# Linear attention: a stacked fp32r gate product, 512-column decay sums, and a moved transpose of y

## The chip, the cores and the metric

The kernel runs on one core of a Trainium2 chip. The metric is the device time of one execution in microseconds (us); lower is better. A core has a matrix engine (TensorE, in profiles PE, its weight loads PEld), a vector engine (VectorE, DVE), a scalar engine (ScalarE, ACT), GpSimd (POOL) and SyncE (SP). Each engine works through its own stream of instructions in order and waits on semaphores for the others. DMA transfers are issued from the queues of SP, ACT and POOL. Matrix products are written to PSUM, a small memory of eight banks of 2 KB for each of 128 partitions; everything else lies in SBUF.

## What is computed

One layer of a streaming encoder is applied to a prompt of 2048 rows and a sample of 32 rows, 1024 channels wide. The mixing part has two branches that are fed by one input projection: banded softmax attention, and gated linear attention (GLA) with 4 heads, keys of 64 and values of 128. A gated MLP with a short convolution follows. The change touches only the linear attention:

```python
log_a = jax.nn.log_sigmoid((gk_low @ p['w_gk2'] + p['b_gk']).astype(jnp.float32)) / GK_NORM
...
cum = jnp.cumsum(ab, axis=2)
cum_end = cum[:, :, -1:]
q_t = qb * jnp.exp(cum) * (dk ** -0.5)
k_t = kb * jnp.exp(-cum)
k_end = kb * jnp.exp(cum_end - cum)
att = jnp.einsum('bnthk,bnshk->bnhts', q_t, k_t) * mask
o_intra = jnp.einsum('bnhts,bnshv->bnthv', att, vb)
upd = jnp.einsum('bnshk,bnshv->bnhkv', k_end, vb)
...
yb = rmsnorm(yb, p['g_gla']) * jax.nn.silu(gb.reshape(b, t, H_B, DV_B))
```

A low-rank product with 16 rows (gk_low) and a bias give a gate for each key channel. Sums of its logarithm over the rows of a block give decays, by which q and k are multiplied. Scores inside a block, a state that is carried on, and a normalisation per head follow.

## The kernel before

The whole program is one Python function, encoder_step. Stages follow each other: the input projection, then the stage of this case, then banded attention, gates and output projection, then the MLP. Of the engines' streams TensorE's is written out by hand (line 82: the order of the code is the order of the stream). On the other engines the framework orders instructions itself. Pools give buffers: bufs is the number of buffers for each tag, and a tile that takes over a buffer waits until the users of the one before are through.

Floating point products of full precision are made in two ways. An F32 operand goes in as it is, and such a product appears in the trace as two TensorE instructions. Or an operand is split into a rounded upper part of type F32R and the rest (split, line 67: a ScalarE copy and a VectorE subtraction), and mm3 (line 74) adds up three products, high by high, high by low and low by high. The projection of q and k of the banded attention does the latter, with 416 columns a product.

**The stage (lines 605 to 830).** Two streams are interleaved on TensorE. One is the generator dense, here qk_stream: 8 groups of weight columns by 5 blocks of 416 rows by 8 steps; one pull is one step, three fp32r products. After each eighth pull a block is complete; t_evac casts it (qh on ScalarE, ql on VectorE) and stores it. The other stream consists of 17 generators gla_chunk(c), for 128 rows each (the last for the 32 sample rows). Each has ten pieces, between the yields. They are numbered here:

1. load of the gate rows gk (L645);
2. transpose of gk to PSUM, and a VectorE copy into the tile gl (L648, L649); row 16 of gl is one and meets the bias row of wgk;
3. loads of v, of the output gate, of q and k; the gate product gl by wgk (L659), and the logarithm of the sigmoid, split into ah and al (L664 to L673);
4. and 5. for p=0 and p=1 (two heads each): the decay sums, products of ah and al with the constant 0/1/-1 matrix cm, in two sets of 320 columns (256 and 128 for the sample rows), each in a PSUM tile ex of the pool pE with two buffers (L682, L683); exponentials into E on ScalarE (L684, L685); decayed copies of k on GpSimd (kd) and VectorE (ke), and of q on VectorE (qd, qi) (L691 to L708);
6. and 7. for p=0 and p=1: scores (L720, L724) into the single tile pa, masked copies into at (L726 to L730), transpose of ke and its copy (L732, L734);
8. and 9. for p=0 and p=1: output products into po (L741, L745) and state update (L750, L753); after p=1 the normalised and gated y (ScalarE L761 to L763, VectorE L764 to L768);
10. transpose of y, a copy, and the store to ybT (L773 to L776).

The pool pM has two buffers, which all of the tiles pz, pz2, ptk, pu and pty use in turn. The columns of cm in order: sums from the block's start up to a row (128), sums from behind a row to the end (128), two coarser levels (64 and 32 rows), and differences against the middle of each 32 rows, 128 columns each.

The loop of lines 811 to 829 sets the order: in step c, cur is chunk c, nxt is c+1, after is c+2, load is c+3. In the order of TensorE the pieces are: 6 of cur; 2 pulls; 3 of nxt; 2 pulls; 7 of cur; 4 pulls; 8 of cur and 4 of nxt; 3 pulls; 9 of cur, 5 of nxt, 2 of after, 1 of load; 6 pulls; 10 of cur.

Of the kernel before, what the change touches and what calls it, by code (L numbers as in the profile page):

```python
# [58 lines left out]
def encoder_step(ctx: ExitStack, tc: tile.TileContext, I, O):  # L59
# [545 lines left out]
    with ExitStack() as st:  # L605
        stq = pool(st, "stgQ", bufs=2)
        gp = pool(st, "gla")
        pE = pool(st, "psE", bufs=2, space=PSUM)
        pA = pool(st, "psA", space=PSUM)
        pM = pool(st, "psM", bufs=2, space=PSUM)  # L610
# [3 lines left out]
        cm = gp.tile([128, 640], F32R, name="cm")  # L614
        cmr = gp.tile([128, 640], F32, name="cmr", tag="E0")
        nc.sync.dma_start(cmr, I["cmat"])
# [5 lines left out]
        wgk = gp.tile([128, 256], F32, name="wgk")  # L622
        nc.vector.memset(wgk, 0.0)
        nc.sync.dma_start(wgk[:17], I["wgk"])
# [10 lines left out]
        gl = gp.tile([128, 128], F32, name="glt")  # L635
        nc.vector.memset(gl, 1.0)

        def gla_chunk(c):
# [10 lines left out]
            nc.vector.tensor_copy(gl[:16, :n], pz[:16, 256:256 + n])  # L649
# [27 lines left out]
            for p in range(2):  # L677
                E = gp.tile([128, 768], F32, name="E", tag=f"E{p}")
                sets = [(0, 256), (512, 640)] if sample else [(0, 320), (320, 640)]
                for a, e in sets:  # L680
                    ex = pE.tile([128, 512], F32, name="ex", tag="ex")
                    nc.tensor.matmul(ex[:, :e - a], ah[:n, 128 * p:128 * p + 128], cm[:n, a:e], start=True, stop=False)  # L682
                    nc.tensor.matmul(ex[:, :e - a], al[:n, 128 * p:128 * p + 128], cm[:n, a:e], start=False, stop=True)  # L683
                    nc.scalar.activation(E[:, a:e], ex[:, :e - a], AF.Exp, scale=1.0 / 16)  # L684
                nc.scalar.activation(E[:, 640:768], ex[:, 512 - a:640 - a], AF.Exp, scale=-1.0 / 16)  # L685
# [5 lines left out]
                nc.gpsimd.tensor_mul(kd[:, :n], k, E[:, 640:640 + n])  # L691
                for j in range(2):
                    hs = slice(64 * j, 64 * j + 64)
                    nc.vector.tensor_mul(qd[hs, p, j, 0:n], q[hs], E[hs, 512:512 + n])
                    if not sample:
                        nc.vector.tensor_mul(qd[hs, p, j, 128:192], q[hs, 64:128], E[hs, 320:384])
# [3 lines left out]
                            E[hs, 384:512].rearrange("p (s c) -> p s c", s=2)[:, :, 32:64])  # L700
                if not sample:
                    nc.gpsimd.tensor_mul(kd[:, 128:192], k[:, 0:64], E[:, 256:320])
# [108 lines left out]
        for c in range(17):  # L811
            cur, nxt, after, load = chunks[c:c + 4]
            step(cur)
            pull(qk_stream, 2)
            step(nxt)
            pull(qk_stream, 2)
            step(cur)
# [1519 lines left out]
```

## Time and profile before

| | us |
|---|---|
| median of 3 runs | 3160.59 (3157.12 to 3160.79) |
| the profiled execution | 3162.02 |
| its span, first to last instruction | 3160.3 |
| VectorE busy in the span | 2239.8 (71%) |
| ScalarE busy in the span | 1648.8 (52%) |
| GpSimd busy in the span | 269.4 (9%) |

All times of the trace come from that one execution and count from the start of its span. A row of the groups or of the order of time names line, engine, operation, and the tiles it writes and reads, with the shape as partitions by elements. Durations of matmuls are modelled, and matmuls that follow each other overlap in the records. Queues, such as ACTq, are the engine's issuing of transfers.

### The profile page before, as it was taken

To read this page: it belongs to the slowest core of one execution; us is meant where nothing else is said; L and a number is where in the kernel's file an instruction comes from. 1 tells how busy PE (TensorE), PEld (TensorE's weight loads), DVE (VectorE), ACT (ScalarE), POOL (GpSimd) and SP (SyncE) were. 2 spreads that over 40 slices of the span, in tenths; PEclk is the share of its full clock that TensorE was granted. 3 is DMA by queue.
4 is the path that set the end of the run, shared out by engine and by line. 5 is a ranking of instruction groups with operands and counts; after the bars stand their busy time and mean duration, and the time that the engine had idled before them with its cause. 6 is when DMAs were issued, how large, how long until landed. Compare 5 with 4: busy or idle time off the path is not lost. (4 is left out here: it accounts for less than half of the span.)

```text
span 3160.3 us, 56426 instructions
## 1 busy us (share of the span) xinstructions
PE 3047.7 (96%) x19748; PEld 2947.7 (93%) x19748; DVE 2239.8 (71%) x4879; ACT 1648.8 (52%) x3792; POOL 269.4 (9%) x427
## 2 busy tenths in 40 slices
PE   6999999999999999999999999999999999999997
PEld 4899999998999999988999899999999999999997
DVE  6735617774555555566677799998888778897877
ACT  4522224443555555544454655567666556576755
POOL 2201201112111111120000000000000000000001
PEclk9999999999999999999999999999999999999998
DMA  7354435554433334575457686788897667888784
GB/s 220 91 156 125 139 98 142 137 137 128 130 109 111 107 100 117 169 230 184 140 175 227 211 256 210 223 256 225 249 265 217 189 189 230 263 250 284 242 267 146
DMA packets 598478, 580.12 MB, mean 184 GB/s; under 512 B 53201, under 2 KB 526530, under 8 KB 598194
## 3 DMA queue, kind: packets, MB, share of 16 engines
q1 hardware_dynamic: 553026, 527.86, 56.2%
q10 hardware_dynamic: 44432, 47.34, 4.7%
q8 instruction: 155, 2.54, 0.3%
q0 software_dynamic: 736, 1.33, 0.2%
q14 instruction: 129, 1.06, 0.1%
HBM read 388.71 MB, written 187.65 MB: 182 GB/s over the span
## 5 line engine op out<-in xcount | busy, mean ns | idle before, releaser
L1882 PE MATMUL ad<-hA,hB 128*128 128x350 f32 (+2 forms) x1734 | 301.7, 324 | 3.8 <-DVE hB L1824 2.4
L1882 PEld LDWEIGHTS ad<-hA,hB 128*128 128x128 f32 x1734 | 282.5, 189 | 5.5 <-DVE hB L1824 3.3
L78 PE MATMUL pm<-hA,wh 128*128 128x416 f32 x768 | 287.4, 374 | 0.0
L79 PE MATMUL pm<-hA,wh 128*128 128x416 f32 x768 | 269.3, 351 | 0.0
L80 PE MATMUL pm<-hA,wl 128*128 128x416 f32 x768 | 269.3, 351 | 0.0
L1824 DVE TENSOR_TENSOR hA<-raws,hA 128x512 fp32r<-128x512 f32 (+1 forms) x367 | 241.9, 668 | 13.0 <-ACT hA L1819 12.7
L1819 ACT ACTIVATE hA<-raws 128x512 fp32r<-128x512 f32 (+1 forms) x367 | 222.0, 617 | 29.9 <-DMA raws<-in_w_up_dram 11.1
L1882 PE MATMUL ad<-hA,hA 128*128 128x348 f32 (+2 forms) x1308 | 225.5, 323 | 2.5 <-ACT work L2008 1.8
L1882 PE MATMUL g<-hA,hB 128*128 128x348 f32 (+2 forms) x1248 | 217.1, 323 | 6.4 <-ACT work L2004 3.5
L1882 PEld LDWEIGHTS ad<-hA,hA 128*128 128x128 f32 x1308 | 211.8, 188 | 3.9 <-ACT work L2008 2.4
L1882 PEld LDWEIGHTS g<-hA,hB 128*128 128x128 f32 x1248 | 202.3, 188 | 9.1 <-ACT work L2004 4.7
L1882 PE MATMUL ad<-hA 128*128 128x350 f32 (+2 forms) x1173 | 205.1, 324 | 4.2 <-DVE hA L1734 4.1
L1882 PEld LDWEIGHTS ad<-hA 128*128 128x128 f32 x1173 | 191.7, 190 | 5.0 <-DVE hA L1734 4.4
L1824 DVE TENSOR_TENSOR hB<-raws,hB 128x512 fp32r<-128x512 f32 (+1 forms) x289 | 190.9, 668 | 6.5 <-ACT hB L1819 6.1
L1819 ACT ACTIVATE hB<-raws 128x512 fp32r<-128x512 f32 (+1 forms) x289 | 175.8, 617 | 25.3 <-DMA raws<-in_w_up_dram 11.8
L69 ACT ACTIVATE pth<-pp 128x256 fp32r<-128x256 f32 (+1 forms) x288 | 106.4, 373 | 139.2 <-PE pp L1027 135.9
L72 DVE TENSOR_TENSOR ptl<-pp,pth 128x256 fp32r<-128x256 f32 (+1 forms) x288 | 118.1, 414 | 85.2 <-ACT pth L69 82.4
L78 PE MATMUL pn<-wh,hA 128*128 128x256 f32 (+1 forms) x624 | 176.9, 283 | 0.0
L79 PE MATMUL pn<-wl,hA 128*128 128x256 f32 (+1 forms) x624 | 176.3, 283 | 0.0
L80 PE MATMUL pn<-wh,hA 128*128 128x256 f32 (+1 forms) x624 | 176.1, 282 | 0.0
L1991 ACT COPY g<-ad 128x348 f32<-128x348 f32 (+2 forms) x102 | 44.3, 434 | 244.1 <-PE ad L1882 156.4
L1882 PE MATMUL g<-hA,hA 128*128 128x350 f32 (+2 forms) x894 | 157.4, 325 | 4.0 <-ACT g L1991 2.3
(507 smaller groups left out, 8468.6 us busy)
## 6 DMA issues: line engine op xcount, KB each, us to landing
raws<-in_w_up_dram SPq DMA_DIRECT2D x220, 256.0 KB, 4.3
raws<-sW SPq DMA_DIRECT2D x176, 256.0 KB, 3.8
sW<-raws SPq DMA_DIRECT2D x88, 256.0 KB, 3.6
raws<-in_w_down_dram SPq DMA_DIRECT2D x80, 256.0 KB, 5.2
wr<-in_w_in_dram SPq DMA_DIRECT2D x76, 256.0 KB, 3.2
sgT<-tx ACTq DMA_DIRECT2D x80, 208.0 KB, 1.9
wa<-in_w_ada_dram SPq DMA_DIRECT2D x64, 256.0 KB, 3.0
keys<-ks SPq DMA_DIRECT2D x128, 128.0 KB, 2.9
```

The source lines that it names most:

```text
L69: i = nc.scalar.activation(hi, src, AF.Copy)
L72: nc.vector.tensor_sub(lo, src, f32(hi))
L78: nc.tensor.matmul(out, ah, bh, start=first and i == 0, stop=False)
L79: nc.tensor.matmul(out, ah, bl, start=False, stop=False)
L80: nc.tensor.matmul(out, al, bh, start=False, stop=last and i == n - 1)
L1819: act = nc.scalar.activation(hi[:, :n], raw(i, n), AF.Copy)
L1824: nc.vector.tensor_sub(lo[:, :n], raw(i, n), f32(hi[:, :n]))
L1882: nc.tensor.matmul(out[:, :w], l_[:, k], r_[:, k, :w], start=first and k == 0 and i == 0, stop=k == n - 1 and i == 2, skip_group_check=True)
L1991: nc.scalar.copy(g[:, 0, :w], ad[:, 0, :w])
```

## The change

Four edits, all in the stage described above.

The gate product: wgk holds three copies of the 17 rows, at partitions 0, 32 and 64: the upper part of the weights twice and their rest once. gl holds the upper part of the gate rows at 0, their rest at 32, the upper part again at 64. One fp32r product then adds up the three products. In piece 2 the transposed rows are copied once from PSUM (gz); two ScalarE copies and a VectorE subtraction fill gl.

The decay sums: the second group of 128 columns is dropped from cm, and the remaining 512 are made in one set, for the sample chunk too. What the dropped columns gave, the decay from a row to the block's end, now comes from a third exponential with a bias tb, the whole block's sum. The order of the columns in E changes with that. The pool pE has one buffer.

The order: piece 10 of chunk c moves into step c+1, behind 6 of cur, 3 of nxt and 2 pulls; 3 of nxt now directly follows 6 of cur.

Buffers: pM has three.

```diff
--- before.py
+++ after.py
@@ -605,23 +605,30 @@
     with ExitStack() as st:
         stq = pool(st, "stgQ", bufs=2)
         gp = pool(st, "gla")
-        pE = pool(st, "psE", bufs=2, space=PSUM)
+        pE = pool(st, "psE", space=PSUM)
         pA = pool(st, "psA", space=PSUM)
-        pM = pool(st, "psM", bufs=2, space=PSUM)
+        pM = pool(st, "psM", bufs=3, space=PSUM)
         pO = pool(st, "psO", space=PSUM)
 
 
-        cm = gp.tile([128, 640], F32R, name="cm")
-        cmr = gp.tile([128, 640], F32, name="cmr", tag="E0")
-        nc.sync.dma_start(cmr, I["cmat"])
+        cm = gp.tile([128, 512], F32R, name="cm")
+        cmr = gp.tile([128, 512], F32, name="cmr", tag="E0")
+        nc.sync.dma_start(cmr[:, 0:128], I["cmat"][:, 0:128])
+        nc.sync.dma_start(cmr[:, 128:512], I["cmat"][:, 256:640])
         nc.vector.tensor_copy(cm, cmr)
         cmask = gp.tile([128, 128], U8, name="cmask")
         cmf = gp.tile([128, 128], F32, name="cmf", tag="qi0")
         nc.sync.dma_start(cmf, I["cmask"])
         nc.vector.tensor_copy(cmask, cmf)
-        wgk = gp.tile([128, 256], F32, name="wgk")
-        nc.vector.memset(wgk, 0.0)
-        nc.sync.dma_start(wgk[:17], I["wgk"])
+        wgk = gp.tile([128, 256], F32R, name="wgk")
+        wgf = gp.tile([128, 256], F32, name="wgf", tag="e1")
+        wgh = gp.tile([128, 256], F32R, name="wgh", tag="ah")
+        nc.vector.memset(wgf, 0.0)
+        for r in (0, 32, 64):
+            nc.sync.dma_start(wgf[r:r + 17], I["wgk"])
+        nc.vector.tensor_copy(wgk[0:64], wgf[0:64])
+        nc.vector.tensor_copy(wgh[64:128], wgf[64:128])
+        nc.vector.tensor_sub(wgk[64:128], wgf[64:128], f32(wgh[64:128]))
         SBP, SBS = [], []
         for p in range(2):
             for x, sb in (("P", SBP), ("S", SBS)):
@@ -632,8 +639,9 @@
         nc.vector.memset(qd, 0.0)
         at = gp.tile([128, 2, 2, 128], F32, name="att")
         nc.gpsimd.memset(at, 0.0)
-        gl = gp.tile([128, 128], F32, name="glt")
-        nc.vector.memset(gl, 1.0)
+        gl = gp.tile([128, 128], F32R, name="glt")
+        for r, v in ((0, 1.0), (32, 0.0), (64, 1.0), (96, 0.0)):
+            nc.vector.tensor_scalar(gl[r:r + 32], onef[r:r + 32], v, None, op0=OP.mult)
 
         def gla_chunk(c):
 
@@ -646,7 +654,11 @@
             yield
             pz = pM.tile([128, 512], F32, name="pz", tag="pm")
             nc.tensor.transpose(pz[:16, 256:256 + n], gk[:n], ident[:n, :n])
-            nc.vector.tensor_copy(gl[:16, :n], pz[:16, 256:256 + n])
+            gz = gp.tile([16, 128], F32, name="gz")
+            nc.vector.tensor_copy(gz[:, :n], pz[:16, 256:256 + n])
+            nc.scalar.activation(gl[0:16, :n], gz[:, :n], AF.Copy)
+            nc.scalar.activation(gl[64:80, :n], gz[:, :n], AF.Copy)
+            nc.vector.tensor_sub(gl[32:48, :n], gz[:, :n], f32(gl[0:16, :n]))
             yield
             vb = gp.tile([128, 512], F32, name="vb", tag="vb", bufs=2)
             nc.sync.dma_start(vb[:n], vn[t0:t0 + n, 512:1024])
@@ -676,35 +688,36 @@
             EX, QI, KE, KD_ = [], [], [], []
             for p in range(2):
                 E = gp.tile([128, 768], F32, name="E", tag=f"E{p}")
-                sets = [(0, 256), (512, 640)] if sample else [(0, 320), (320, 640)]
-                for a, e in sets:
-                    ex = pE.tile([128, 512], F32, name="ex", tag="ex")
-                    nc.tensor.matmul(ex[:, :e - a], ah[:n, 128 * p:128 * p + 128], cm[:n, a:e], start=True, stop=False)
-                    nc.tensor.matmul(ex[:, :e - a], al[:n, 128 * p:128 * p + 128], cm[:n, a:e], start=False, stop=True)
-                    nc.scalar.activation(E[:, a:e], ex[:, :e - a], AF.Exp, scale=1.0 / 16)
-                nc.scalar.activation(E[:, 640:768], ex[:, 512 - a:640 - a], AF.Exp, scale=-1.0 / 16)
+                ex = pE.tile([128, 512], F32, name="ex", tag="ex")
+                nc.tensor.matmul(ex, ah[:n, 128 * p:128 * p + 128], cm[:n], start=True, stop=False)
+                nc.tensor.matmul(ex, al[:n, 128 * p:128 * p + 128], cm[:n], start=False, stop=True)
+                tb = gp.tile([128, 1], F32, name="tb", tag=f"tb{p}")
+                nc.scalar.activation(tb, ex[:, n - 1:n], AF.Copy, scale=1.0 / 16)
+                nc.scalar.activation(E[:, 0:512], ex, AF.Exp, scale=1.0 / 16)
+                nc.scalar.activation(E[:, 512:640], ex[:, 384:512], AF.Exp, scale=-1.0 / 16)
+                nc.scalar.activation(E[:, 640:640 + n], ex[:, 0:n], AF.Exp, bias=tb, scale=-1.0 / 16)
                 EX.append(E)
                 q, k = qk[:, 0, p, :n], qk[:, 1, p, :n]
                 qi = gp.tile([128, 128], F32, name="qi", tag=f"qi{p}")
                 ke = gp.tile([128, 128], F32, name="ke", tag=f"ke{p}")
                 kd = gp.tile([128, 256], F32, name="kd", tag=f"kd{p}")
-                nc.gpsimd.tensor_mul(kd[:, :n], k, E[:, 640:640 + n])
+                nc.gpsimd.tensor_mul(kd[:, :n], k, E[:, 512:512 + n])
                 for j in range(2):
                     hs = slice(64 * j, 64 * j + 64)
-                    nc.vector.tensor_mul(qd[hs, p, j, 0:n], q[hs], E[hs, 512:512 + n])
+                    nc.vector.tensor_mul(qd[hs, p, j, 0:n], q[hs], E[hs, 384:384 + n])
                     if not sample:
-                        nc.vector.tensor_mul(qd[hs, p, j, 128:192], q[hs, 64:128], E[hs, 320:384])
+                        nc.vector.tensor_mul(qd[hs, p, j, 128:192], q[hs, 64:128], E[hs, 192:256])
                         nc.vector.tensor_mul(
                             qd[hs, p, j, 192:256].rearrange("p (s c) -> p s c", s=2),
                             q[hs].rearrange("p (s c) -> p s c", s=2)[:, :, 32:64],
-                            E[hs, 384:512].rearrange("p (s c) -> p s c", s=2)[:, :, 32:64])
+                            E[hs, 256:384].rearrange("p (s c) -> p s c", s=2)[:, :, 32:64])
                 if not sample:
-                    nc.gpsimd.tensor_mul(kd[:, 128:192], k[:, 0:64], E[:, 256:320])
+                    nc.gpsimd.tensor_mul(kd[:, 128:192], k[:, 0:64], E[:, 128:192])
                     nc.gpsimd.tensor_mul(
                         kd[:, 192:256].rearrange("p (s c) -> p s c", s=2),
                         k.rearrange("p (s c) -> p s c", s=2)[:, :, 0:32],
-                        E[:, 384:512].rearrange("p (s c) -> p s c", s=2)[:, :, 0:32])
-                nc.vector.tensor_mul(ke[:, :n], k, E[:, 128:128 + n])
+                        E[:, 256:384].rearrange("p (s c) -> p s c", s=2)[:, :, 0:32])
+                nc.vector.tensor_mul(ke[:, :n], k, E[:, 640:640 + n])
                 nc.vector.tensor_mul(qi[:, :n], q, E[:, 0:n])
                 QI.append(qi)
                 KE.append(ke)
@@ -811,8 +824,10 @@
         for c in range(17):
             cur, nxt, after, load = chunks[c:c + 4]
             step(cur)
+            step(nxt)
             pull(qk_stream, 2)
-            step(nxt)
+            if c:
+                step(chunks[c - 1])
             pull(qk_stream, 2)
             step(cur)
             pull(qk_stream, 4)
@@ -824,7 +839,8 @@
             step(after)
             step(load)
             pull(qk_stream, 6 if c < 16 else 1 << 20)
-            step(cur)
+            if c == 16:
+                step(cur)
             if c == 15:
                 state_io(SBP, O["gla_prompt"], True)
         state_io(SBS, O["gla_sample"], True)
```

## Prediction

> **What bounds the kernel now.** I read the page first, then the windows view cut at the starts of one line, then the waits, then the order of time.
>
> ```profile
> PE 3047.7 (96%) x19748; PEld 2947.7 (93%) x19748; DVE 2239.8 (71%) x4879; ACT 1648.8 (52%) x3792; POOL 269.4 (9%) x427
> ```
> ```profile
> 465.25:780.70 315.45, 310.91 (x1703) 287.88 (x1702) 212.18 (x745) 142.87 (x492) 52.32 (x119) 1.00 0.49 130
> 491.04:509.14 18.10, 16.93 (x94) 15.62 (x93) 12.73 (x45) 7.95 (x29) 2.57 (x6) 1.00 0.52 139
> 593.18:609.53 16.35, 16.35 (x93) 15.59 (x93) 11.82 (x44) 7.64 (x28) 2.59 (x6) 1.00 0.51 135
> 491.04:744.20 253.16, 250.14 (x1382) 233.44 (x1381) 187.48 (x661) 121.71 (x428) 40.12 (x92) 1.00 0.49 130
> ```
> ```profile
> PE pty L773 <- DVE y L768: 2.7, 3, 1.2
> ```
>
> A row of the windows view gives the stretch, its length, then busy time and count of TensorE, its weight loads, VectorE, ScalarE and GpSimd, and after them the granted clock. The change lies wholly in the linear-attention stage, 315 us of the span (first row). TensorE sets the time there: its share is 99%, at full clock. I cut the stage where each chunk's output product (L741, p=0) starts. One undisturbed chunk takes 16.35 us with TensorE busy throughout; fifteen chunks take 253.16, so 253.16 - 15 x 16.35 = 7.9 us is excess. The first chunk shows 1.75 of it, and the wait that the view names is the transpose of y for the DVE's y. So there are two things to gain: shorter streams of TensorE, and these waits. Since TensorE is never spare, every microsecond that it streams less or waits more moves the end by as much.
>
> **What the TensorE edits save.** In the order of time a row has start, duration, engine, line, operation, out<-in, shapes and count. Recorded matmuls overlap, so I price one by the distance of starts in a run, not by its duration.
>
> ```profile
> 596.77 0.59 PE L741 MATMUL po<-SBP,qi 128*128 128x256 f32 x2
> ...
> 598.22 0.31 PE L683 MATMUL ex<-cm,al 128*128 128x320 f32 x1
> 598.37 0.31 PE L682 MATMUL ex<-cm,ah 128*128 128x320 f32 x1
> ...
> 602.18 0.60 PE L773 MATMUL pty<-ident,y 128*128 128x128 f32 x4
> 602.62 0.60 PE L720 MATMUL pa<-qbd,kd 128*128 128x256 f32 x2
> ...
> 603.78 0.35 PE L79 MATMUL pm<-hA,wh 128*128 128x416 f32 x1
> 603.97 0.35 PE L80 MATMUL pm<-hA,wl 128*128 128x416 f32 x1
> ...
> 604.53 0.35 PE L80 MATMUL pm<-hA,wl 128*128 128x416 f32 x1
> 604.72 0.59 PE L659 MATMUL pz<-wgk,glt 128*128 128x256 f32 x2
> ...
> 605.34 0.36 PE L79 MATMUL pm<-hA,wh 128*128 128x416 f32 x1
> ```
> ```profile
> 300.03 0.28 PE L80 MATMUL pn<-wh,hA 128*128 128x256 f32 x1
> 300.15 0.28 PE L78 MATMUL pn<-wh,hA 128*128 128x256 f32 x1
> ...
> 301.57 0.40 PE L501 MATMUL pw<-acch,pick 128*2 128x512 f32 x1
> 301.80 0.39 PE L502 MATMUL pw<-accl,pick 128*2 128x512 f32 x1
> ```
>
> Gate product: from 604.53 to 605.34 lie two 416-column matmuls at 0.19 and the product, 0.81 - 0.38 = 0.43. An fp32r product of 256 columns steps by 0.12 (300.03 to 300.15). That saves 0.31 in each of 17 chunks: **-5.3**. The stacking costs nothing here: one product of 128 rows does all three partial products. If the fp32r form saved nothing, this term would be 0.
>
> Decay sums: eight matmuls a chunk at 0.15 (598.22 to 598.37) become four of 512 columns at 0.23 (301.57 to 301.80): 1.18 - 0.92 = 0.26, by 16 chunks -4.2; the sample chunk, whose four pairs were only 256 and 128 columns, pays some 0.2. **-4.0**.
>
> The Trainium skill, "TensorE: Matmul & The Clock Gate", section "Back-to-back issue gap", gives 131 ns per matmul as the sustained pace at 512 columns. By that the sums would save about 10 us, an estimate from that page; the row's 0.23 speaks against it, and I go by the row.
>
> The y wait: its place moves behind p=0's scores, the gate product and two pulls of the qk stream (six matmuls at 0.19, 1.13). Scores p=0 take 602.62 to 603.78 - 0.19, thus 0.97. Together 2.2 us later, more than the longest wait of 1.2: I let the whole excess go: **-7.9** (some of it has other causes, so up to 2 us of it may stay).
>
> **What is late next.** The gate product of the next chunk used to come after the y transposes, p=0's scores and two pulls. Now it directly follows the scores. It used to need one DVE copy (L649); now it needs that copy, two ScalarE copies and then a DVE subtraction into rows 32 to 47. Where does that subtraction get its place?
>
> ```profile
> 599.02 0.28 DVE L649 COPY glt<-pz 16x128 f32<-16x128 f32 x1
> 599.67 0.29 DVE L707 TENSOR_TENSOR ke<-qk,E 128x128 f32<-128x128 f32 x1 [0.38 <-ACT E L684]
> ...
> 602.77 0.22 DVE L697 TENSOR_TENSOR qbd<-qk,E 64x64 f32<-64x64 f32 x1
> 603.02 0.59 DVE L72 TENSOR_TENSOR ql<-pm,qh 128x416 fp32r<-128x416 f32 x1
> ```
> ```profile
> 599.22 0.42 ACT L684 ACTIVATE E<-ex 128x320 f32<-128x320 f32 x1
> 599.54 0.19 ACT L763 ACTIVATE ss<-ss 128x4 f32<-128x4 f32 x1
> 599.63 0.43 ACT L684 ACTIVATE E<-ex 128x320 f32<-128x320 f32 x1
> ...
> 600.11 0.53 ACT L69 ACTIVATE qh<-pm 128x416 fp32r<-128x416 f32 x1
> ```
>
> From 599.67 to 602.99 VectorE works without a gap on y and on p=1's decayed q and k. The copy L649 slipped in ahead because its input was there. The ql subtraction (L72) is the telling row: its input qh ended at 600.64, yet it ran at 603.02, when the older work was through. The new subtraction stands in the program between that work and ql, and its input comes at about the same time: the ScalarE copies stand behind p=1's exponentials. I put it where ql is, just ahead of it.
>
> Now the working for that chunk, in time from L741 p=1 (596.77). The transposes started at +5.41; with 0.14 less for p=1's sums the scores start at +5.27 and TensorE reaches the gate product at **+6.25**. The VectorE stretch ended at +6.22. It starts later now: the 512-column exponential ends some 0.19 after one of 320 (192 columns at the step of these rows, 0.32 for 320), and the tiny bias copy ahead of it costs 0.1 like L763 (599.54 to 599.63); together 0.29. The subtraction takes 0.28 like L649 (0.22 if it is like L697), its signal 0.05. So it ends at 6.22 + 0.62 = **+6.84**, and TensorE waits 0.6. An undisturbed chunk saves 0.31 + 0.26 and gives it all back.
>
> ```profile
> 494.65 0.59 PE L741 MATMUL po<-SBP,qi 128*128 128x256 f32 x2
> ...
> 730.91 0.59 PE L741 MATMUL po<-SBP,qi 128*128 128x256 f32 x2
> ```
> ```profile
> 502.18 0.22 DVE L697 TENSOR_TENSOR qbd<-qk,E 64x64 f32<-64x64 f32 x1
> ...
> 736.91 0.22 DVE L697 TENSOR_TENSOR qbd<-qk,E 64x64 f32<-64x64 f32 x1
> ```
>
> Over 15 such chunks (first and last shown) the stretch ends between +6.22 and +7.75, 6.57 in the mean. The first one ends at +7.75, because it was late for y as well: the lateness that held the transposes holds the gate product instead. New wait: 15 x (6.57 + 0.62 - 6.25) = **+14.1**. Its ends: 0 if the subtraction comes early, 19 if the stretch grows by another 0.3. Behind the waiting product on TensorE stand two pulls, the transposes and p=1's scores; ScalarE's gate functions wait for it, with two pulls and the transposes more time before the sums than before.
>
> Start of the stage, once:
>
> ```profile
> 470.53 1.28 ACTq L216 DMA_DIRECT2D qs<-qh  x2
> ...
> 479.39 0.29 ACT L685 ACTIVATE E<-ex 128x128 f32<-128x128 f32 x1
> ```
> ```profile
> 472.73 0.59 PE L659 MATMUL pz<-wgk,glt 128*128 128x256 f32 x2
> ...
> 479.40 0.30 PE L682 MATMUL ex<-cm,ah 128*128 128x320 f32 x1
> ```
>
> The first chunk's two gate copies queue behind DMA issues that end at 471.81; with the subtraction and three more DVE operations on wgk the product comes 0.3 to 1.3 late. With one buffer for the sums, p=1's, at 479.40, must wait for exponentials that end at 479.68 or later: 0.3 to 1.2. I take **+1.4** for both. The three extra DMAs on SP's queue cover nothing that is late there; the gate product's four loads, and SP's stream behind them, move by two pulls, and their users come eight pulls later; the ybT store on ScalarE's queue moves with y. The third PSUM buffer of pM costs nothing; it holds the gate output, which ScalarE and VectorE still read while y and a key block are transposed. With two buffers the y transposes would have to wait for the end of those gate functions.
>
> The rest is hidden. ScalarE gains two gate copies and a bias copy for each p and loses little on the exponentials, some 0.7 us a chunk beside 7.64 busy of 16.35. GpSimd's products and VectorE's ke now wait for a second or third exponential instead of a first, a few tenths later; their users are the scores, some 6 us on for p=0 and 9 for p=1. Without that cover each tenth would be paid in each chunk.
>
> Sum: -5.3 - 4.0 - 7.9 + 14.1 + 1.4 = -1.7. The profiled execution took 3162.02 (span 3160.3), 1.4 over the median 3160.59: 3160.3 there, **3158.9** on the median. A measurement tells about 0.2%, 6.3 us, from no change.
>
> **Rivals.** (1) The subtraction comes early, between the older VectorE operations, as L649 did; TensorE never waits for it. For: its input could be there by 600.7, 2.3 us ahead of need. Against: ql's row. Then -5.3 - 4.0 - 7.9 + 1.4 = -15.8: **3144.8**. Half-way cases lie between.
>
> (2) Slower: the single buffer of the decay sums. p=1's sums wait until all exponentials of p=0 are through.
>
> ```profile
> 494.66 0.63 ACT L191 ACTIVATE wh<-wr 128x512 fp32r<-128x512 f32 x1 [0.36 <-PE pm L79]
> 495.20 0.50 ACT L209 ACTIVATE qh<-pm 128x416 fp32r<-128x416 f32 x1
> ...
> 495.73 1.50 ACTq L216 DMA_DIRECT2D qs<-qh  x2
> ...
> 596.16 0.29 ACT L685 ACTIVATE E<-ex 128x128 f32<-128x128 f32 x1
> ```
>
> They end at 596.45 and p=1 starts at 597.89: 1.44 us of room, little changed, since two of 320 and one of 128 give way to one of 512 and two of 128. It decides if a finished qk block's cast and its DMA issues (0.5 + 1.5) and a weight cast (0.63) get ahead of them: 2.6 - 1.44 = 1.2 us in the 6 of 16 chunks where a block ends in those three pulls (a block is eight pulls, so in three chunks of eight), and 0.6 more in half of these, where a second weight cast does too: 7.2 + 1.8 = 9, so **3168**. In the row they came after. The Trainium skill, "PSUM — Partial Sum Buffer", section "PSUM bank collisions raise a hardware error", says that a bank must not be written while another engine reads it; so this wait can't be left out, and no run here shows its cost.
>
> (3) The fp32r gate is no cheaper: 3164.
>
> **Chances.** Forecast 0.55, own range 3153 to 3165; rival 1 0.24, the cases between 0.08; rival 2 0.10; rival 3 0.03. Faster by over 0.2% (under 3154.3): rival 1, the between cases and 0.04 of the forecast, 0.36. Slower (over 3166.9): rival 2 and a wait grown past 19 us, 0.12. Same 0.52. Range 3144 to 3167: from rival 1 to the edge of rival 2.
>
> **What would show it.** Undisturbed chunks at 16.3 us with TensorE idle about 0.6 ahead of L659's successor, released by VectorE's write of glt, and none at pty: right. Chunks at 15.8: rival 1. Waits of ex for E: rival 2. A gate product stepping 0.43: rival 3. The forecast is wrong if the new subtraction stands ahead of y on VectorE.

## The result and the profile after

| | us |
|---|---|
| before, median of 6 runs | 3159.81 (3156.66 to 3162.68) |
| after, median of 6 runs | 3171.82 (3168.84 to 3177.29) |
| after to before | 1.004 (95% interval 1.003 to 1.005) |
| the profiled execution after | 3171.06 (span 3169.4) |

The change makes the kernel slower by 12 us. The forecast was 3158.9 with a range up to 3167: the sign and the size are both off.

First the windows view of the changed kernel, with the columns as in the prediction. The rows are the stage (last product of the projection to the first score of the next stage), the first chunk and an undisturbed one, and fifteen chunks. The chunks are cut at the output product of p=1 (now L754); the prediction cut at that of p=0, by which the fifteen take 261.8.

```profile
461.10:784.91 323.81, 304.21 (x1620) 278.82 (x1618) 223.86 (x768) 154.67 (x558) 48.50 (x121) 0.99 0.48 128
491.73:511.64 19.91, 17.59 (x88) 16.29 (x88) 13.84 (x48) 9.24 (x34) 2.29 (x7) 0.91 0.46 123
599.73:616.56 16.83, 16.11 (x89) 14.89 (x89) 12.42 (x46) 8.74 (x32) 2.40 (x7) 1.00 0.45 118
491.73:753.87 262.14, 244.18 (x1307) 225.66 (x1306) 197.53 (x679) 132.64 (x488) 36.72 (x94) 0.99 0.48 127
```

The stage takes 323.8 us where it took 315.6 by the same cut (the prediction's row begins 0.1 later). TensorE was busy in all of an undisturbed chunk before (16.35 of 16.35); now it is busy for 16.11 of 16.83. It streams less, as meant, and stands still for more than that. The first chunk grew from 18.1 to 19.9, and its row shows a clock of 0.91, which no chunk of before did. The waits view of TensorE in this stage names the cause in one line:

```profile
PE pz L671 <- DVE glt L661: 18.0, 15, 2.6
PE ex L692 <- ACT E L698: 0.6, 1, 0.6
PE pz L656 <- DMA gk<-vn: 0.4, 1, 0.4
```

The gate product waits for VectorE's subtraction 15 times, 18.0 us together, 2.6 at the longest. The waits of y's transposes (2.7 us before) are gone. So the wait moved, as the prediction said; it is far larger than the one that it replaced. The order of time in the undisturbed chunk, TensorE first, then VectorE:

```profile
605.92 0.27 PE L745 MATMUL ptk<-ident,ke 128*128 128x128 f32 x1
606.91 0.35 PE L671 MATMUL pz<-wgk,glt 128*128 128x256 f32 x1 [0.72 <-DVE glt L661]
607.11 0.34 PE L78 MATMUL pm<-hA,wh 128*128 128x416 f32 x1
```
```profile
602.80 0.28 DVE L707 TENSOR_TENSOR qbd<-qk,E 64x128 f32<-64x128 f32 x1 [0.43 <-ACT E L696]
...
604.43 1.12 DVE L781 SCALAR_TENSOR_TENSOR y<-po,ss,sg 128x128 f32<-128x128 f32 x4
...
606.17 0.28 DVE L721 TENSOR_TENSOR qi<-qk,E 128x128 f32<-128x128 f32 x1
606.49 0.28 DVE L661 TENSOR_TENSOR glt<-gz,glt 16x128 fp32r<-16x128 f32 x1
606.80 0.59 DVE L72 TENSOR_TENSOR ql<-pm,qh 128x416 fp32r<-128x416 f32 x1
```

The subtraction (L661) stands where the forecast put it: last in VectorE's stretch of work, just ahead of ql. The two ScalarE copies ahead of it (their rows below) were through at 603.79; it waited for its turn on VectorE, not for data. The stretch itself begins with a wait for the 512-column exponential (L696).

```profile
603.16 0.29 ACT L659 ACTIVATE glt<-gz 16x128 fp32r<-16x128 f32 x1
603.48 0.31 ACT L660 ACTIVATE glt<-gz 16x128 fp32r<-16x128 f32 x1
```

The first chunk adds something that the forecast did not have:

```profile
500.48 0.43 PE L671 MATMUL pz<-wgk,glt 128*128 128x256 f32 x1 [2.32 <-DVE glt L661]
500.70 0.55 PE L78 MATMUL pm<-hA,wh 128*128 128x416 f32 x1
501.05 0.55 PE L79 MATMUL pm<-hA,wh 128*128 128x416 f32 x1
...
504.20 0.35 PE L80 MATMUL pm<-hA,wl 128*128 128x416 f32 x1
504.39 0.35 PE L78 MATMUL pm<-hA,wh 128*128 128x416 f32 x1
```
```profile
500.48:503.99 3.51, 3.51 (x13) 3.29 (x13) 1.96 (x7) 1.47 (x5) 0.00 (x0) 0.52 0.53 149
```

After the wait of 2.32 us the 416-column products step by 0.35 instead of 0.19, for some 3.4 us; the windows row shows a granted clock of 0.52 there. This wait cost about 1.6 us more than itself.

Something more lies outside the stage. In the MLP, a thousand microseconds later, a product waits longer for ScalarE's work, and ScalarE for a load of weights. The rows of before come first, then those of after:

```profile
1862.61 0.63 ACT L1819 ACTIVATE hA<-raws 128x512 fp32r<-128x512 f32 x1 [2.31 <-DMA raws<-in_w_up_dram]
```
```profile
1863.63 4.12 PE L1882 MATMUL ad<-hA,hB 128*128 128x350 f32 x24 [0.49 <-ACT work L2008]
```
```profile
1867.52 0.63 ACT L1835 ACTIVATE hA<-raws 128x512 fp32r<-128x512 f32 x1 [4.01 <-DMA raws<-in_w_up_dram]
```
```profile
1868.54 1.76 PE L1898 MATMUL ad<-hA,hB 128*128 128x350 f32 x7 [2.18 <-ACT work L2024]
```

The stretch around it, from the first product g of hB to the first of hB by hB, took 294.3 us before and 298.0 after. The spans of the two profiled executions differ by 9.1 us: 4.0 less ahead of the stage, 8.2 more in it and 4.9 more behind it, of which 3.7 lie in this stretch. One pair of profiles does not show that the parts outside the stage belong to the change. The code ahead of the stage is the same in all kernels and took 461.1 to 467.5 us in the sixteen profiles, and the code behind it took 2379.6 us in this profile of before and 2387.2 in a second one (before_again). So 8.2 of the 12 us are traced to the stage; what the rest is comes up again under the late weight load.

### The profile page after: what moved, and what is told of

It reads as the page before. It is cut to its first block, busy times and chain, and to the rows that moved or that the text cites. A ratio compares the mean times of both kernels' runs of the same rounds, so it can differ in the third digit from the quotient of the medians.

```text
span 3169.4 us, 56407 instructions
## 1 busy us (share of the span) xinstructions
PE 3042.0 (96%) x19663; PEld 2939.5 (93%) x19663; DVE 2252.2 (71%) x4902; ACT 1661.9 (52%) x3860; POOL 263.6 (8%) x427
## 5 line engine op out<-in xcount | busy, mean ns | idle before, releaser
L1835 ACT ACTIVATE hB<-raws 128x512 fp32r<-128x512 f32 (+1 forms) x289 | 175.8, 617 | 29.2 <-DMA raws<-in_w_up_dram 14.1
```

Of the source, the lines that this page charges most:

```text
L1835: act = nc.scalar.activation(hi[:, :n], raw(i, n), AF.Copy)
```

## The experiments

Each group of experiments had its own runs of the kernel before on the same chip, and each ratio stands to those (their medians: 3165.8 for the first four runs, 3168.0 for the next four, 3163.4 and 3164.9 for the last two groups). The stage and the MLP stretch are from one profile each.

| kernel | median, us | ratio to before, 95% interval | stage, us | MLP stretch, us |
|---|---|---|---|---|
| before | 3159.81 | | 315.6 | 294.3 |
| after | 3171.82 | 1.004 (1.003 to 1.005) | 323.8 | 298.0 |
| gate_late | 3163.85 | 0.9986 (0.9977 to 0.9996) | 308.8 | 296.0 |
| sub_pool | 3161.27 | 0.9981 (0.9972 to 0.9991) | 306.1 | 297.1 |
| gate_f32 | 3160.61 | 0.9985 (0.9975 to 0.9994) | 307.3 | 299.3 |
| decay_only | 3176.24 | 1.0029 (1.0017 to 1.0041) | 323.6 | 299.5 |
| stacked_only | 3164.67 | 0.9991 (0.9982 to 1.0001) | 312.1 | 295.5 |
| sub_pool_later | 3159.61 | 0.9974 (0.9965 to 0.9983) | 304.2 | 300.2 |
| wait_longer | 3232.35, one run | | 377.8 | 299.4 |
| before_again | 3167.9, one run | | 314.7 | 294.6 |
| after_split | 3174.01 | 1.0033 (1.0023 to 1.0042) | 318.9 | 298.9 |
| decay_split | 3171.64 | 1.0023 (1.0013 to 1.0033) | 319.8 | 299.5 |
| best_split | 3154.43 | 0.9971 (0.9959 to 0.9982) | 302.0 | 298.1 |
| before_plus1 | 3164.08 | 1.0001 (0.9992 to 1.001) | 315.6 | 296.1 |
| best_plus1 | 3157.04 | 0.9976 (0.9967 to 0.9985) | 304.7 | 299.7 |
| best_minus1 | 3153.28 | 0.9967 (0.9955 to 0.998) | 300.9 | 299.0 |

**Is it the wait for the subtraction?** Three kernels take that wait away in three ways. The first moves the gate product (piece 3 of the next chunk) back behind the two pulls, its place before the change:

```diff
             step(cur)
-            step(nxt)
             pull(qk_stream, 2)
+            step(nxt)
             if c:
                 step(chunks[c - 1])
```

> The changed kernel with the gate product of the next chunk back behind two pulls (six matmuls at 0.19, 1.13 us later than in the changed kernel), all else kept. Stage means from the last product of the input projection to the first score of the banded attention: 315.6 us before, 323.8 after. Theory A (TensorE waits at the gate product for the subtraction into glt, which stands last in VectorE's stretch, and the two longest waits cost half clock as well): the 15 waits of 0.5 to 2.6 us lose 1.1 us each, the two of over 2.3 fall to 1.3 to 1.5 and the half clock goes; stage about 304, time about 3151. Theory B (the loss comes from the single PSUM buffer of the decay sums, or from outside the stage): waits at the gate product go, but the stage stays above 315 and the time above 3165.

The stage falls by 15 us. What is left are 5.0 us of waits for glt, 1.4 the longest, and no half clock:

```profile
PE pz L671 <- DVE glt L661: 5.0, 8, 1.4
```

The second leaves the order and gives the subtraction to GpSimd:

```diff
-            nc.vector.tensor_sub(gl[32:48, :n], gz[:, :n], f32(gl[0:16, :n]))
+            nc.gpsimd.tensor_sub(gl[32:48, :n], gz[:, :n], f32(gl[0:16, :n]))
```

> The changed kernel with the subtraction into glt on GpSimd in place of VectorE; order, gate product and decay sums kept. Theory A (place in VectorE's stretch): GpSimd has only p=1's three products ahead of it, about 4.3 us behind L754 p=1, the gate product comes at 6.3; waits gone but for some tenths in the first and third chunk; stage about 301, time about 3149. If the wait were for the ScalarE copies (ending 4.1 behind) or for the transpose of gk, nothing would change: stage 324, 3172. Theory B (single PSUM buffer, or outside the stage): above 3165.

The undisturbed chunk falls to 15.82 us, 0.53 less than before. GpSimd takes twice as long for the subtraction, but is through with it over a microsecond ahead of need (one row of GpSimd, then the gate product, which follows the transpose of ke with no wait):

```profile
596.77 0.58 POOL L661 TENSOR_TENSOR glt<-gz,glt 16x128 fp32r<-16x128 f32 x1
```
```profile
598.50 0.27 PE L745 MATMUL ptk<-ident,ke 128*128 128x128 f32 x1
598.52 0.36 PE L671 MATMUL pz<-wgk,glt 128*128 128x256 f32 x1
```

What is late next is the score product of p=1, which waits for the masked copies of p=0's scores:

```profile
PE pa L733 <- DVE att L743: 3.2, 4, 1.6
```

The third undoes the stacking: gate product in F32, one copy, everything else as changed.

```diff
-            gz = gp.tile([16, 128], F32, name="gz")
-            nc.vector.tensor_copy(gz[:, :n], pz[:16, 256:256 + n])
-            nc.scalar.activation(gl[0:16, :n], gz[:, :n], AF.Copy)
...
+            nc.vector.tensor_copy(gl[:16, :n], pz[:16, 256:256 + n])
```

> The changed kernel with the F32 gate product of before (glt filled by one VectorE copy, two TensorE instructions, 0.43 us), new order, decay sums and buffers kept. Theory A: no subtraction, so no wait at the gate product, at 0.31 us more in 17 chunks: stage about 305, time about 3153. Theory B: above 3165.

Stage 307.3 and no wait at the gate product. So the other two edits, the sums and the moved y, gain 8 us by themselves, and adding the stacked product to them costs 16.5, although it streams 0.31 less a chunk. All three agree: the subtraction's place on VectorE is the loss in the stage. Some waiting is left here too, for the masked copies:

```profile
PE pa L722 <- DVE att L732: 2.1, 2, 1.6
```

**What does each part do alone?** decay_only is the kernel before with the 512-column sums (and the PSUM buffers that go with them), in the old order and with the F32 gate.

```diff
-            step(nxt)
             pull(qk_stream, 2)
-            if c:
-                step(chunks[c - 1])
+            step(nxt)
             pull(qk_stream, 2)
...
-            if c == 16:
-                step(cur)
+            step(cur)
```

(This diff is against the changed kernel; the gate is undone as above.)

> The kernel before with only the decay sums in 512 columns (single PSUM buffer, third exponential, three pM buffers), order and gate product of before. From rows: 0.26 us less in 16 chunks, 0.6 more once at the start for the single buffer; the y waits of before stay. Theory A: stage about 312, time about 3157. Theory B in its form that the single buffer is the loss: stage above 318, time above 3162.

This was the surprise. The sums alone, which the prediction priced at -4.0, cost the stage 8 us. TensorE does stream less, but y comes later, and its transposes wait. The waits view, then VectorE around y in the first chunk of before and of decay_only (their p=1 output products start at 494.65 and 495.42):

```profile
PE pty L775 <- DVE y L770: 8.6, 7, 2.1
```
```profile
500.56 0.29 DVE L694 TENSOR_TENSOR qbd<-qk,E 64x128 f32<-64x128 f32 x1
500.88 1.13 DVE L768 SCALAR_TENSOR_TENSOR y<-po,ss,sg 128x128 f32<-128x128 f32 x4
```
```profile
501.79 0.16 DVE L768 SCALAR_TENSOR_TENSOR ss<-ss 128x4 f32<-128x4 f32 x1
501.98 0.22 DVE L699 TENSOR_TENSOR qbd<-qk,E 64x64 f32<-64x64 f32 x1
502.24 1.12 DVE L770 SCALAR_TENSOR_TENSOR y<-po,ss,sg 128x128 f32<-128x128 f32 x4
```

y starts 6.23 us after the output product before, and 6.82 after it here. Two of the waits at the transposes grow past 1.8 us, and both are followed by the half clock.

stacked_only is the kernel before with the stacked gate product alone; for want of room its tile gz shares the buffer of kn0.

```diff
-            gz = gp.tile([16, 128], F32, name="gz")
+            gz = gp.tile([16, 128], F32, name="gz", tag="kn0")
```

> The kernel before with only the stacked fp32r gate product (gz shares the buffer of kn of p=0 for want of room), old order, old decay sums, two buffers each. Theory A (the loss needs the gate product close behind the scores, and decay sums that make VectorE's stretch later): the gate product comes 1.1 us later than in the changed kernel, so hardly a wait for glt; 0.31 saved in 17 chunks, some of the y waits of before 0.1 to 0.3 longer: stage about 311 against 315.6, time 0.9985 of before. Theory B (the stacked gate product is bad in itself, by its ScalarE copies): stage above 318.

The undisturbed chunk falls from 16.35 to 16.03, and the y waits stay as they were; the stage gains 3.5 us. In the old order the gate product has time enough: two pulls and the y transposes more.

**How much does the exponential's length do?** after_split and decay_split cut the long exponential of the two kernels in two, the half that VectorE reads first in front, and put the small bias copy behind both:

```diff
-                nc.scalar.activation(tb, ex[:, n - 1:n], AF.Copy, scale=1.0 / 16)
-                nc.scalar.activation(E[:, 0:512], ex, AF.Exp, scale=1.0 / 16)
+                nc.scalar.activation(E[:, 256:512], ex[:, 256:512], AF.Exp, scale=1.0 / 16)
+                nc.scalar.activation(E[:, 0:256], ex[:, 0:256], AF.Exp, scale=1.0 / 16)
+                nc.scalar.activation(tb, ex[:, n - 1:n], AF.Copy, scale=1.0 / 16)
```

> The changed kernel, with the 512-column exponential of each decay sum in two of 256 columns, the half that the decayed q reads first, and the small bias copy behind both. Theory (a part of the new wait comes from the decay sums, because VectorE's stretch now starts behind one long exponential): the stretch starts and ends 0.3 us earlier, the wait of the gate product for the subtraction falls from 0.95 to about 0.65 us in the undisturbed chunks, whose period falls from 16.8 to 16.5; the two long waits fall from 2.3 and 2.6 to 2.0 and 2.3, and one of them may no longer be followed by the half clock; the stage falls from 323.8 to 317 to 320 us. Rival (the stretch's end is set by y and its inputs, or by the subtraction's place alone): the start of the stretch does not matter, period 16.8, stage 323 to 325.

> The kernel before with the 512-column decay sums alone (as in decay_only), with the same split of the exponential. Theory (the sums alone cost 8 us because the longer exponential and the bias copy put y off on VectorE): y comes 0.3 us earlier, the waits at its transposes fall from 1.88 and 2.09 to about 1.6 and 1.8, at least one half clock goes, and the stage falls from 323.6 to 314 to 319 us. Rival (the cost is on TensorE or from the single buffer of the sums): stage 323 to 325.

In after_split the wait falls from 0.72 to 0.53 in the record of an undisturbed chunk, the period from 16.8 to 16.57, and the stage by 4.9: the longer exponential is a part of the loss, but the smaller one. decay_split falls by 3.8, a little less than expected (319.8 against 314 to 319). The other 4 us over before are then not the exponential's length alone. They are still waits for y: its transposes wait six times, 6.6 us together, where before has three, 2.7 together, and one of the six is followed by half clock. What keeps y late there is not shown.

```profile
PE pty L776 <- DVE y L771: 6.6, 6, 1.7
```

The median of after_split did not follow its stage (ratio 1.0033 against 1.004 for the changed kernel, with intervals that overlap).

**What does a longer wait cost?** wait_longer makes the subtraction four times, with the same values:

```diff
-            nc.vector.tensor_sub(gl[32:48, :n], gz[:, :n], f32(gl[0:16, :n]))
+            for _ in range(4):
+                nc.vector.tensor_sub(gl[32:48, :n], gz[:, :n], f32(gl[0:16, :n]))
```

> The changed kernel with the subtraction into glt made four times over, the same values each time, so 0.3 x 3 = 0.9 us more in VectorE's stretch ahead of the gate product. Theory A without the clock: 15 waits longer by 0.9, stage 323.8 + 13.5 = 337. Theory A with the clock (waits of 1.9 and more bring half clock for some 3 us, at a cost of about 1.6; those up to 1.6 don't): five more chunks cross that line, stage about 345. If the gate product's wait had another cause than this subtraction: 324.

The stage took 377.8, 33 us over the upper end of what was expected. Two things were missed. VectorE did not run the four in a row: the framework put ql and two masked copies between them, so the wait grew by 2.2 us instead of 0.9. And each of the fifteen waits is now followed by half clock. VectorE, then TensorE, in an undisturbed chunk:

```profile
608.75 0.28 DVE L662 TENSOR_TENSOR glt<-gz,glt 16x128 fp32r<-16x128 f32 x1
609.07 0.59 DVE L72 TENSOR_TENSOR ql<-pm,qh 128x416 fp32r<-128x416 f32 x1
609.69 0.28 DVE L662 TENSOR_TENSOR glt<-gz,glt 16x128 fp32r<-16x128 f32 x1
610.00 0.30 DVE L740 COPY_PREDICATED att<-cmask,pa 128x128 f32<-128x128 uint8 x1
610.33 0.28 DVE L662 TENSOR_TENSOR glt<-gz,glt 16x128 fp32r<-16x128 f32 x1
...
610.98 0.28 DVE L662 TENSOR_TENSOR glt<-gz,glt 16x128 fp32r<-16x128 f32 x1
```
```profile
611.40 0.55 PE L672 MATMUL pz<-wgk,glt 128*128 128x256 f32 x1 [2.96 <-DVE glt L662]
611.76 0.55 PE L78 MATMUL pm<-hA,wh 128*128 128x416 f32 x1
612.10 0.55 PE L79 MATMUL pm<-hA,wh 128*128 128x416 f32 x1
```

Such a chunk takes 20.6 us against 15.8 with no wait at all. The difference of 4.8 is the recorded wait of 2.96, some 0.25 that the record does not count (it counts from the modelled end of the transpose ahead, 0.27 us after its start; where nothing waits, the product starts 0.02 after it), and 1.6 for the half clock.

**Does the chip matter?** before_again is the kernel before, profiled on the chip of stacked_only, sub_pool_later and wait_longer.

> The kernel before, unchanged, for its three stretches on the same chip as the other runs of this call: stage 315.6. If the stretch behind the stage (2379.6 in the first profile of before, 2384.5 in that of the changed kernel, 2387 to 2388 in four experiments) differs by the chip alone, it is within 2 us of the other runs of this call; if the changed stage alters what follows, it is 3 to 8 us shorter than theirs.

Stage 314.7 and MLP stretch 294.6: the two stretches on which the argument rests hold from chip to chip within 1 us, though the whole execution took 5.9 us more than the first profiled one. Behind the stage it took 2387.2 us, as in the four experiments that the expectation names, and not 3 to 8 us less: the length of that whole stretch says nothing about the change.

**Is there a version that gains?** sub_pool_later is sub_pool with the scores of p=1 one pull later, so that the masked copies of p=0 are through.

```diff
-            pull(qk_stream, 2)
+            pull(qk_stream, 3)
             step(cur)
-            pull(qk_stream, 4)
+            pull(qk_stream, 3)
```

> The changed kernel with the subtraction into glt on GpSimd, and p=1's scores one pull later (3 and 3 pulls around them in place of 2 and 4). With the subtraction on GpSimd alone the waits left in 15 chunks were those of p=1's scores for the att copies (1.08 and 1.61 in the first and third chunk, 0.2 to 0.3 in some), each shorter by one pull, 0.57: stage about 303.5 against 306.1. Theory A: time about 0.997 of before. Rival: p=1's products then wait for att instead and nothing is gained, stage 306 or more.

The stage falls to 304.2, and the waits for the masked copies from 3.2 to 1.6 us. best_split adds the split exponential:

> The best version so far (the changed kernel with the subtraction on GpSimd and p=1's scores one pull later), with the same split of the exponential. Theory: in the undisturbed chunks TensorE already waits for nothing, so only the first three chunks and the bumps of the others can gain: stage 304.2 falls to 302 to 304, ratio to before 0.997. Rival: the two extra ScalarE instructions of each chunk hold up the gate functions, stage 304 to 306.

302.0 us, eleven of sixteen chunks between 15.76 and 15.85. The waits left on TensorE are these; all but the one for att lie ahead of the first chunk's output products:

```profile
PE pz L656 <- DMA gk<-vn: 1.3, 1, 1.3
PE pa L734 <- DVE att L744: 0.8, 1, 0.8
PE ex L692 <- ACT E L699: 0.7, 1, 0.7
PE pz L671 <- POOL glt L661: 0.3, 1, 0.3
```

**The late weight load of the MLP.** The three profiles without the new sums showed 294.3 to 295.5 us in the MLP stretch, the nine with them 296.0 to 300.2 (wait_longer's not counted). They also differ in the number of loads issued at the stage's start. Three kernels change that number, by loading cmat in one DMA more (before_plus1, best_plus1) or one less (best_minus1, which for that also casts it in two pieces):

```diff
-        nc.sync.dma_start(cmr, I["cmat"])
+        nc.sync.dma_start(cmr[:, 0:128], I["cmat"][:, 0:128])
+        nc.sync.dma_start(cmr[:, 128:640], I["cmat"][:, 128:640])
```

> The kernel before with the load of cmat in two DMAs instead of one, nothing else. What is open: some 3.7 us of the loss lie a thousand us behind the edited stage, in one stretch of the feed-forward stage (from the first product g of hB to the first of hB by hB), 294.3 to 295.5 us in the three profiles of kernels without the new decay sums, 296.0 to 300.2 in the nine with them; there a product waits for a weight load that lands later. Those three kernels issue 0 or 2 loads more than before in the edited stage's start, the nine 1 or 3. Theory (the number of DMAs ahead decides how the later loads fall on the DMA engines): this kernel, with 1 more, shows 296 to 300 us in that stretch and is 2 to 4 us slower than before, its edited stage staying at 315. Rival (it belongs to the new sums themselves, whatever the count): 294 to 295.5 us and no difference.

> best_split with the load of cmat in three DMAs instead of two, which makes 4 more than before. Theory of the count of DMAs: the stretch of the feed-forward stage falls from 298.1 to 294 to 295.5 us, the time to 0.996 of before. Rival (the new sums themselves): 296 to 300 us, ratio 0.997 as best_split.

> best_split with the load of cmat in one DMA as before (all 640 columns, cast in two pieces), which makes 2 more than before. Theory of the count of DMAs: as best_plus1, 294 to 295.5 us in that stretch and 0.996 of before. Rival (the new sums themselves): 296 to 300 us, ratio 0.997.

The theory of the count falls: 299.7 and 299.0 us with the sums, whatever the number of loads. Without them, before_plus1 shows 296.1, the lower edge of what that theory expected, but no difference in time. The stretch goes mostly with the sums (296.0 to 300.2 in twelve profiles with them, wait_longer included, 294.3 to 296.1 in four without); the two ranges touch, and each is one profile per kernel. The medians speak for a loss outside the stage all the same: by their ratios, the eleven kernels with the sums that ran several times are 1.1 to 7.1 us slower than the change of their stage alone would make them, 3.6 in the mean, and the two without (stacked_only, before_plus1) 0.7 and 0.3. A single ratio is uncertain by some 3 us, but all eleven lie on the same side. How an edit of this stage costs time behind it, in the MLP or elsewhere, stays open. best_minus1 is the fastest kernel of all, 0.9967 of before (0.9955 to 0.998); since its interval overlaps those of best_split, best_plus1 and sub_pool_later, only its gain over before is shown, not that over these.

## Why the prediction was wrong

- **What bounds the stage: right.** TensorE is never spare there; each microsecond of its waits showed at the end of the stage.
- **Gate product (-5.3): right.** 16.35 to 16.03 in an undisturbed chunk of stacked_only is 0.32, against 0.31. Rival 3 (no cheaper in fp32r) is out.
- **Decay sums (-4.0): right for TensorE alone.** Both edits together bring the undisturbed chunk to 15.8 where nothing waits (sub_pool_later, best_split), 0.55 less than 16.35, against 0.57. The step of the 512-column product is again 0.23 (597.81 to 598.04 in the order of time of the changed kernel), so the 131 ns that the Trainium skill gives ("TensorE: Matmul & The Clock Gate", section "Back-to-back issue gap") do not show here either. But the sums are not a saving by themselves: decay_only loses 8 us.
- **The y wait (-7.9): right that it goes, too large as a gain.** No wait for y is left in the changed kernel. But where the wait for the subtraction is taken away as well, other waits appear that neither before nor the changed kernel shows: in gate_f32 fifteen chunks take 245.3 us (cut at p=0) where 15 of 16.1, its undisturbed length, would make 241.5. So about 4 of the 7.9 us stay, more than half of them as the waits for the masked copies shown above, twice the 2 us that the forecast allowed. In the changed kernel this does not show; there the new wait and its half clock make up the whole excess, as worked out next.
- **The place of the new wait: right.** The subtraction stands last in VectorE's stretch, just ahead of ql. Rival 1 (it slips in early) did not happen on VectorE; on GpSimd it did, and sub_pool's stage, 9.5 us under that of before, shows what it would have been worth there.
- **The size of the new wait (+14.1): this is the step that failed.** An undisturbed chunk was to stay at 16.35 us and took 16.8. Fifteen chunks of 15.78 us without any wait make 236.7; the profile has 261.8 (cut at p=0), so the wait cost 25 us. The forecast had the stretch end at 6.57 + 0.29 = 6.86 us after the output product, in the mean of 15 chunks; it ended at 7.18. It shifted the old ends by a constant 0.29, as if the stretch only started later. In the undisturbed chunks it began only 0.17 later (602.80 is 3.07 after its output product, 599.67 was 2.90), but the same twelve operations, with ke and qi last instead of first, took 3.65 instead of 3.32: it ended at 6.72 (forecast 6.51). In the two worst chunks it ended at 8.29 and 8.55, where 7.75 had been the latest before. The subtraction's end came to the product's start in 0.15 us, not 0.05, and TensorE was ready at 6.19 (the transpose of ke at 6.17 in the mean, 0.02 more as in sub_pool's rows), not 6.25. The product started at 7.64 in the mean, so the wait is 7.64 - 6.19 = 1.45 us instead of 0.94 (6.57 + 0.62 - 6.25), by 15 chunks 21.7 (the waits view, which leaves out 0.25 of each, has 18.0). The half clock after the waits of 2.32 and 2.59 adds 2 times 1.6 = 3.2. That makes 24.9.
- **The upper end of the range.** "19 if the stretch grows by another 0.3" was nearly what happened (21.7). With the half clock on top, 24.9, the prediction's own sum gives 3169.7, past 3167 before anything outside the stage is counted.
- **The start (+1.4): right in sum.** From the stage's start to the first output product it took 25.9 us before and 27.1 after.
- **Rival 2 (the single buffer of the sums)** showed once in the profile, 0.6 us at the start; it isn't the loss.
- **What lies behind the stage** was not in the forecast at all: by the medians 3.8 us (12.0 less 8.2), of which the profile has 3.7 in the MLP stretch. Its cause stays open.

The sum of the stage, from the profile: -15 x 0.57 = -8.6 for the shorter streams, -7.9 for y, +25.1 for the new wait, +1.2 at the start and -1.6 at the end make +8.2. Most of the -1.6 at the end is no gain of the change: the first profile of before waits 1.48 us there for a load of q, before_again 0.45.

## What to carry to other kernels

When a wait is moved away from a product, ask which product becomes the next to need the same engine: here VectorE's stretch was late for y, and the change put another product, with an operation queued at the end of that same stretch, into the place that y left. A small operation that another engine waits for can be better placed on an engine that is idle, even if it runs there at half the speed: here the subtraction took 0.58 us on GpSimd against 0.28 on VectorE, and moving it gained 18 us in the stage. And a saving on the bounding engine that lengthens an operation feeding a crowded one should be tried with that engine's order shown, not priced by streams alone.

## What the runs showed of the hardware

**The clock falls after short waits.** Waits of TensorE of some 2 us can be followed by half its clock for 3.4 us. Over this stage in all the profiles, no single wait of up to 1.56 us was; of the ten between 1.57 and 2.18, four were (1.57, 1.88, 2.09, 2.10) and six were not (1.59, 1.61, 1.62, 1.66, 1.98, 2.18); from 2.3 on, every one was. The first row here is after_split's, with no drop, to set beside the 2.32 of the changed kernel above:

```profile
503.04 0.35 PE L671 MATMUL pz<-wgk,glt 128*128 128x256 f32 x1 [2.18 <-DVE glt L661]
503.23 0.35 PE L78 MATMUL pm<-hA,wh 128*128 128x416 f32 x1
```

But short waits add up. In best_plus1 two waits of 1.13 and 0.66 us, with 1.5 us of work between them, were followed by half clock:

```profile
482.89 0.50 PE L693 MATMUL ex<-cm,ah 128*128 128x512 f32 x1 [1.13 <-ACT ah L69]
485.08 0.50 PE L693 MATMUL ex<-cm,ah 128*128 128x512 f32 x1 [0.66 <-ACT E L700]
```
```profile
482.12:485.53 3.41, 1.98 (x7) 1.27 (x8) 0.68 (x3) 1.56 (x6) 0.00 (x0) 1.00 0.99 319
485.53:488.94 3.41, 3.41 (x12) 3.19 (x11) 3.34 (x15) 1.66 (x6) 2.14 (x6) 0.50 0.81 236
```

The trace's record of the granted clock shows what counts. Each stretch of half clock lasts 3.41 us, two of wait_longer's 6.83, and within a run they start whole multiples of 3.41 apart (500.61 and 538.16 in the changed kernel, eleven times 3.41). Cut on this grid, in the six profiles with such a drop, every window of the stage with over 2.0 us of recorded idle time of TensorE was followed by half clock, and no window at full clock with under 1.4 was; between these, 1.43 (the row above), 1.57 and 1.88 were and 1.48, 1.49, 1.53 and 1.92 were not. The wait of 2.18 had no effect because an edge of the grid cut it into 1.92 and 0.26.

The Trainium skill, "TensorE: Matmul & The Clock Gate", Part 1, section "What's actually happening", lets the clock fall to half after an idle window of about 3.4 us that runs freely, and its table in "Why this matters for your kernels" asks for no gaps over about 3 us. The 3.41 us and the fixed grid agree with the window; that it has to be idle throughout does not: here 1.4 to 2.6 us of idle time in it were enough.

**Repeated operations need not run back to back.** In wait_longer the framework ran other work between the four subtractions, so doubling a cost in the code is no measure of that cost unless the order of time shows where the copies went.
